# A Mamba-2 scan taken two chunks at a time, with sigmoids from the hyperbolic tangent and one logarithm per group norm

## The chip, the core and the metric

One core of a Trainium2 chip runs the whole kernel in one launch. The metric is device time in microseconds (us) of that core. "Before" is the kernel as it stood, "after" the changed one. Lines L... are lines of the kernel's file; those of before and after differ by up to some twenty.

## What is computed

A step of a two-layer network on 1024 prompt tokens and 32 new ones (together 1056; the kernel lays them out as 1060 columns, with a gap of four). Layer 0 has a Mamba-2 mixer, layer 1 latent attention; after each comes an embedding with a sigmoid gate. The mixer, which is the part that most of the change touches:

```python
def ssd_mixer(hn, conv_prev, h0, chunk, in_w, conv_w, conv_b, dt_bias, A_log, Dp, norm_w, out_w):
    proj = hn @ in_w
    z, xbc, dt = jnp.split(proj, [SSD_D_INNER, SSD_D_INNER + SSD_CONV_DIM], axis=-1)
    xbc, conv_new = causal_conv(xbc, conv_prev, conv_w, conv_b)
    xbc = jax.nn.silu(xbc)
    ...
    dt = jax.nn.softplus((dt + dt_bias).astype(F32)).reshape(b, T, SSD_GROUPS, SSD_HPG)
    A = -jnp.exp(A_log.astype(F32)).reshape(SSD_GROUPS, SSD_HPG)
    ...
    y, hT = ssd_scan(xs, dt, A, Bm, Cm, h0, chunk)
    y = y + Dp.reshape(SSD_GROUPS, SSD_HPG)[..., None] * xs
    y = y.reshape(b, T, SSD_D_INNER) * jax.nn.silu(z)
    y = rmsnorm(y.reshape(b, T, SSD_GROUPS, SSD_D_INNER // SSD_GROUPS), ...)
    out = (y @ out_w).astype(hn.dtype)
...
def ple(h, p, up_w, norm_w, gate_w):
    g = jax.nn.sigmoid((rmsnorm(h, norm_w) @ gate_w).astype(F32)).astype(h.dtype)
    return (p @ up_w).astype(h.dtype) * g
```

In the scan, with the running sums Acs of dt * A in a chunk, a chunk's own part is y_diag = (C B^T * exp(Acs_l - Acs_s) * dt, lower triangle) x, and the part from before is y_off = C h * exp(Acs); the state goes on as h * exp(Acs_last) + B^T (decay * dt * x). The kernel's chunks are of 128 tokens (eight, and the 32 new tokens as a ninth).

## The kernel before, in words

Tokens lie along the free axis, features on the partitions. float32 products are made in three parts: an operand is split into a high and a low half (h, l; wh, wl), and hh*wh, hl*wh, hh*wl are added up (`gemm`, L211 to L217). Weights come by DMA as wraw; ScalarE rounds them to wh (L206), GpSimd subtracts to wl (L207).

`phase_ssd` takes 8 groups of 4 heads. A group has six weight blocks of 128 columns: B, C, two x blocks, and two z blocks. `mblock` multiplies one block by the normalised input in three column tiles (384, 384, 292), 24 products each, so 72 products a block; ScalarE copies each tile from PSUM into a buffer raw (L335). `conv_block` makes the convolution of width 4 and SiLU from raw (ScalarE L415, VectorE three times L417, `sigmoid` L188 to L191, multiply L420). `gate` does the same for z and multiplies y by it on GpSimd (L427, L430). `scan_group` goes over the nine chunks: three transposes and C B^T into tile tr (L454 to L457), xd and xe (L464, L465), bt (L466), cbm (L467), four subtractions dm (L470), an exponential (L472), a multiply (L473), the products y_off and y_diag into yp (L477, L480), the new state st (L482), and the sums (L485 to L497). `finish` makes a group's norm, column tile by column tile: Square (L510), an add on GpSimd (L512), a split into ysh and ysl (L222, L223), two products with ones into psy (L261, L262), Ln and Exp (L182, L183), and the weighted multiply (L521).

The program's order is: blocks of group 0 and the first scan; then per group g the scan of g, the blocks B and C of g+1, the gates of g-1, x block 0 of g+1, the norm of g-1 (`finish`), x block 1 of g+1. In place of the blocks of a ninth group the last group has its gates and `up_product` for the embedding (144 products).

Ahead of it all stands the time-step chain (L358 to L404): softplus by a series on VectorE, the running sum, and nine transposes of the 96-row tile stk (pstk, L403), whose copies tokT (L404) hold dt, Acs and decay by token; every scan needs them.

The framework orders each engine's instructions once, when the kernel is built, and every engine then runs its own list in order. PSUM buffers are handed out by tag, in the order of the program: the next tile of a tag waits until the one that had its buffer has been read. Before, products (tag mm) have three banks, tr two, yp, st and "n" (the norms' sums, pstk, psy) one each.

Of the kernel before, what the change touches and what calls it, by code (L numbers as in the profile page):

```python
# [17 lines left out]
P = 128  # L18

T1 = 1060  # L20
RAWB = 7
# [133 lines left out]
class Pools:  # L155
    """tile pools by tag"""
# [29 lines left out]
def sigmoid(nc, out, x):  # L186
    """1 / (1 + exp(-x)); the cap on exp(-x) only keeps it finite"""
    nc.scalar.activation(out, x, AF.Exp, scale=-1.0)  # L188
    nc.vector.tensor_scalar(out, out, 1e30, None, op0=ALU.min)  # L189
    nc.scalar.activation(out, out, AF.Ln, bias=1.0)  # L190
    nc.scalar.activation(out, out, AF.Exp, scale=-1.0)  # L191
# [39 lines left out]
def up_product(c, i, piece, raw, tiles, ps_tile, evac, nb=1):  # L231
    """p @ W_up of layer i for one piece of the tokens, to DRAM"""
# [26 lines left out]
def ones_sum(c, ps, h, l):  # L259
    """column sums of h + l, to all rows"""  # L260
    c.nc.tensor.matmul(ps, c.ones_r, h, start=True, stop=False)  # L261
    c.nc.tensor.matmul(ps, c.ones_r, l, start=False, stop=True)  # L262


def phase_ssd(c, ctx):
# [17 lines left out]
    with tc.tile_pool(name="xin", bufs=2, side="right") as xp:  # L283
        def busy(x, k):
            """keeps the tensor engine's clock up while it waits for data; the products are not used"""
            ps = pt.tile([P, 512], F32, tag="tr", name="busy")
            for _ in range(k):
                nc.tensor.matmul(ps[:, : x.shape[-1]], c.ones, x, start=True, stop=True)

        busy(c.ones, 10)  # L290
        for j, (o, n) in enumerate(TILES1):
# [6 lines left out]
            ps = pn.tile([P, 512], F32, tag="n", name=f"psn{j}")  # L298
# [22 lines left out]
    def mblock(*blocks, ws=None):  # L321
        """products of weight blocks (source, columns, evacuation) with all tiles of hn, tile by tile"""
# [26 lines left out]
    # time steps  # L349
    with tc.tile_pool(name="dt", bufs=1) as dp:  # L350
# [57 lines left out]
    def conv_block(wsrc, b, raw=None):  # L408
# [9 lines left out]
        th = raw[:, 0:T1]  # L418
        sigmoid(nc, th, xh)
        nc.vector.tensor_tensor(xh, th, xh, op=ALU.mult)  # L420
        return xh

    def gate(g, b, S):
        z = raw_block(I["inW"][6 * g + 4 + b])[:, 3:]
        th = kp.tile([P, 3 + T1], F32, tag="raw", name="zs", bufs=RAWB)[:, 3:]
        sigmoid(nc, th, z)
        nc.gpsimd.tensor_tensor(z, th, z, op=ALU.mult)  # L427
        for j, (o, n) in enumerate(TILES1):
            yb = S["y"][j][:, b, :n]
            nc.gpsimd.tensor_tensor(yb, yb, z[:, o : o + n], op=ALU.mult)  # L430

    def scan_group(g, S):
        hT = None
        ys = S["y"] = []
        for j in range(3):
            y = wk.tile([P, 2, 384], F32, tag="y", name=f"y{j}", bufs=6)
            ys.append(y)
        nc.gpsimd.memset(ys[2][:, :, 256:260], 0.0)
        for ch in range(9):
            o, L = (ch * 128, 128) if ch < 8 else (SMP1, 32)  # L440
            j = min(ch // 3, 2)
            oy = o - TILES1[j][0]
            cs = slice(o, o + L)
            if ch == 8:
# [3 lines left out]
            ab = wk.tile([P, 4, 128], F32, tag="ab", name="ab", bufs=2)  # L448
            nc.sync.dma_start(ab[:L, :, :L], acs_d[4 * g : 4 * g + 4, cs].partition_broadcast(L))
            eb = wk.tile([P, 2, 128], F32, tag="eb", name="eb", bufs=2)  # L450
            for hf in range(2):
                nc.sync.dma_start(eb[64 * hf : 64 * hf + 64, :, :L], ea_d[4 * g + hf : 4 * g + 4 : 2, cs].partition_broadcast(64))
            tr = pt.tile([P, 512], F32, tag="tr", name="tr")
            nc.tensor.transpose(tr[:L, 0:128], S["x"][0][:, cs], c.ident)  # L454
            nc.tensor.transpose(tr[:L, 128:256], S["x"][1][:, cs], c.ident)
            nc.tensor.transpose(tr[:L, 256:384], S["B"][:, cs], c.ident)
            nc.tensor.matmul(tr[:L, 384 : 384 + L], S["B"][:, cs], S["C"][:, cs], start=True, stop=True)  # L457
            xv = tr[:L, 0:256].rearrange("p (h q) -> p h q", q=64)
            xd = wk.tile([P, 256], F32, tag="xd", name="xd", bufs=2)
            xe = wk.tile([P, 256], F32, tag="xe", name="xe", bufs=2)  # L460
            bt = wk.tile([P, 128], F32, tag="bt", name="bt", bufs=2)
            cbm = wk.tile([P, 128], F32, tag="cbm", name="cbm", bufs=2)
            hs = slice(4 * g, 4 * g + 4)
            nc.vector.tensor_tensor(xd[:L].rearrange("p (h q) -> p h q", q=64), xv, bc_last(tokT[:L, ch, 4 * g : 4 * g + 4], 64), op=ALU.mult)  # L464
# [1000 lines left out]
```

## Time and profile before

| | us |
|---|---|
| median of 3 runs | 2060.45 |
| lowest and highest run | 2057.85, 2061.4 |
| span of the profiled execution | 2062.5 |

The profiled execution has no time apart from its span. A row of a group reads: line, engine, operation, written tile <- read tiles, size, count, then busy us and mean ns of one, then idle time of the engine ahead of it and what ended most of it. A row of a timeline starts with start and length in us. "A <- B: us, n, longest" in the waits is the time that A waited for B.

### The profile page before, as it was taken

Reading aid. Unit: us, or ns where it says so; the run is one execution under the profiler, and the core shown is the slowest. Engines: PE = TensorE matmul, PEld = TensorE weight load, DVE = VectorE, ACT = ScalarE, POOL = GpSimd, SP = SyncE. Lnnn points to the kernel's source line nnn. Section 1 sums busy time; section 2 is a strip of 40 time slices with the busy share of each in tenths; the row PEclk is TensorE's granted clock in tenths of the full one; section 3 lists DMA queues with packets and bytes.
Section 4 is the critical chain, followed back from the end, with each engine's and each line's share of the span. In section 5 each row is a group of like instructions: output and inputs, shape, how many; then the busy total and the mean of one; then the engine's idle time right before and its main releaser. Section 6 shows DMA issues by size and latency. Waiting matters only on the chain. (4 is left out here: it accounts for less than half of the span.)

```text
span 2062.5 us, 33817 instructions
## 1 busy us (share of the span) xinstructions
PE 1961.9 (95%) x12871; PEld 1788.2 (87%) x12871; DVE 1426.8 (69%) x2158; ACT 1114.9 (54%) x1954; POOL 1022.9 (50%) x861
## 2 busy tenths in 40 slices
PE   7999998999999998999999899999899999989998
PEld 5988898999989997999999899877777777779998
DVE  7867888887988988435257645364679787886555
ACT  4443645456454555534244535487587767754343
POOL 5432636454563546554577544122446353655772
PEclk8999999999999999999999999999999999999999
DMA  3115253443425354735333222432612221325432
GB/s 126 52 49 109 70 107 68 93 86 78 106 61 109 64 126 126 244 118 184 102 99 120 84 70 91 144 107 84 141 29 73 60 75 32 105 64 180 132 115 79
DMA packets 141457, 204.33 MB, mean 99 GB/s; under 512 B 20272, under 2 KB 93488, under 8 KB 141168
## 3 DMA queue, kind: packets, MB, share of 16 engines
q1 hardware_dynamic: 136192, 193.18, 34.7%
q0 software_dynamic: 2800, 6.91, 1.8%
q8 instruction: 101, 1.65, 0.3%
q10 hardware_dynamic: 2304, 2.10, 0.3%
q14 instruction: 60, 0.49, 0.1%
HBM read 156.81 MB, written 38.83 MB: 95 GB/s over the span
## 5 line engine op out<-in xcount | busy, mean ns | idle before, releaser
L207 POOL TENSOR_TENSOR wl<-wraw,wh 128x1024 fp32r<-128x1024 f32 (+2 forms) x185 | 389.9, 2109 | 491.1 <-ACT wh L206 456.7
L217 PE MATMUL mm<-hh,wh 128*128 128x384 f32 (+3 forms) x1176 | 385.3, 328 | 5.4 <-ACT raw L335 5.2
L217 PE MATMUL mm<-hl,wh 128*128 128x384 f32 (+3 forms) x1176 | 388.4, 331 | 0.0
L217 PE MATMUL mm<-hh,wl 128*128 128x384 f32 (+3 forms) x1176 | 386.4, 329 | 0.0
L206 ACT ACTIVATE wh<-wraw 128x1024 fp32r<-128x1024 f32 (+3 forms) x183 | 158.7, 868 | 248.8 <-PE pso L217 124.1
L217 PE MATMUL pso<-yhl,wh 128*128 128x264 f32 x1536 | 285.0, 286 | 3.7 <-DVE yhl L223 2.0
L217 PEld LDWEIGHTS pso<-yhl,wh 128*128 128x128 f32 x1536 | 240.6, 190 | 5.0 <-DVE yhl L223 2.7
L217 PEld LDWEIGHTS mm<-hh,wh 128*128 128x128 f32 (+1 forms) x1176 | 220.9, 188 | 10.9 <-ACT raw L335 5.8
L217 PEld LDWEIGHTS mm<-hl,wh 128*128 128x128 f32 (+1 forms) x1176 | 221.2, 188 | 5.2 <-issue 2.5
L217 PEld LDWEIGHTS mm<-hh,wl 128*128 128x128 f32 (+1 forms) x1176 | 220.9, 188 | 4.7 <-issue 2.1
L217 PE MATMUL pso<-yhl,wl 128*128 128x264 f32 x768 | 219.8, 286 | 4.0 <-POOL wl L207 4.0
L217 PE MATMUL psi<-yhl,wh 128*128 128x264 f32 (+1 forms) x896 | 168.7, 289 | 4.2 <-DVE t L692 3.2
L217 PEld LDWEIGHTS pso<-yhl,wl 128*128 128x128 f32 x768 | 145.8, 190 | 4.5 <-POOL wl L207 4.5
L417 DVE SCALAR_TENSOR_TENSOR cx<-raw,pv,cx 128x1060 f32<-128x1060 f32 x96 | 141.4, 1498 | 11.6 <-ACT cx L415 11.5
L217 PE MATMUL pg<-hH,wl 128*128 128x264 f32 x512 | 146.0, 285 | 3.3 <-POOL wl L207 3.3
L217 PE MATMUL pg<-hH,wh 128*128 128x264 f32 x512 | 145.9, 285 | 0.0
L217 PE MATMUL pg<-hL,wh 128*128 128x264 f32 x512 | 145.6, 285 | 0.0
L217 PEld LDWEIGHTS psi<-yhl,wh 128*128 128x128 f32 (+1 forms) x896 | 139.3, 187 | 6.3 <-ACT lsH L222 3.2
L1228 PE MATMUL st<-qk 128*128 128x512 f32 (+2 forms) x576 | 139.6, 358 | 1.3 <-DMA qk<-mr 0.6
L217 PE MATMUL psi<-yhl,wl 128*128 128x264 f32 (+1 forms) x448 | 130.7, 292 | 2.8 <-POOL wl L207 2.8
L1249 POOL TENSOR_TENSOR pl<-pf,ph 128x512 fp32r<-128x512 f32 x64 | 81.0, 1266 | 104.0 <-DVE ph L1248 97.5
L470 DVE TENSOR_SCALAR dm<-ab,tokT 128x128 f32<-128x128 f32 (+1 forms) x288 | 120.8, 476 | 11.3 <-DMA ab<-acs_d 8.2
(522 smaller groups left out, 4866.4 us busy)
## 6 DMA issues: line engine op xcount, KB each, us to landing
wraw<-in_inW SPq DMA_DIRECT2D x48, 512.0 KB, 4.1
ab<-acs_d SPq DMA_DIRECT2D x64, 256.0 KB, 5.0
wraw<-in_outW SPq DMA_DIRECT2D x32, 512.0 KB, 3.8
yraw<-y_d SPq DMA_DIRECT2D x32, 264.0 KB, 4.6
u<-u_d SPq DMA_DIRECT2D x32, 264.0 KB, 2.7
eb<-ea_d SPq DMA_DIRECT2D x128, 64.0 KB, 3.4
wraw<-in_gateW SPq DMA_DIRECT2D x16, 512.0 KB, 3.5
wraw<-in_oW SPq DMA_DIRECT2D x16, 512.0 KB, 3.6
```

The source lines that it names most:

```text
L206: nc.scalar.activation(wh, raw, AF.Copy)
L207: nc.gpsimd.tensor_tensor(wl, raw, wh.bitcast(F32), op=ALU.subtract)
L217: c.nc.tensor.matmul(ps, ww[:, k, :m], aa, start=first and k == 0 and i == 0, stop=last and k == n - 1 and i == 2)
L417: nc.vector.scalar_tensor_tensor(xh, raw[:, k : k + T1], pvc(c, "cw", 4 * b + k), xh, op0=ALU.mult, op1=ALU.add)
L470: nc.vector.tensor_scalar(dm[:L, h, :L], ab[:L, h, :L], tokT[:L, ch, 32 + 4 * g + h : 33 + 4 * g + h], 0.0, op0=ALU.subtract, op1=ALU.min)
L1228: nc.tensor.matmul(ps[:, :n], a_[:, ks], b_[:, q], start=t == 0, stop=t == 2)
L1249: (nc.gpsimd if idx in L_POOL else nc.vector).tensor_tensor(pl[:, :n], pf[:, :n], ph[:, :n].bitcast(F32), op=ALU.subtract)
```

## The change

Four things are done:

- The scan takes chunks in pairs (`for q in range(5)`, the ninth alone). The four subtractions and the exponential of a chunk become one subtraction over 128x1024 with operands spread by broadcast, a Relu and an Exp; xd, xe, bt, cbm, the sums and the loads are made for two chunks at once. PSUM has three mm banks as before, and one bank each for trx, trb, yd, yf and st. pstk and psy, which had the bank "n", are now tiles of tag mm.
- Sigmoid and SiLU come from the hyperbolic tangent: sigmoid(x) = (1 + tanh(x/2))/2, one ScalarE pass and one VectorE operation. The halves are folded into the convolution's weights (cw, cb), the norm's weights (snw; the norm's scale becomes 1/1024) and the embedding's last operation.
- The z multiply moves from GpSimd to VectorE, and the multiply of y by z is one operation per block.
- `finish` copies the three sums into one tile r of 1060 columns and takes one Ln and one Exp over it. The tables of ScalarE's functions are loaded by ACT_TABLE_LOAD: 1 before, 30 after.

The core of the diff (the added lines of the scan without those that they replace):

```diff
-RAWB = 7
+RAWB = 6
...
-def sigmoid(nc, out, x):
-    """1 / (1 + exp(-x)); the cap on exp(-x) only keeps it finite"""
-    nc.scalar.activation(out, x, AF.Exp, scale=-1.0)
-    nc.vector.tensor_scalar(out, out, 1e30, None, op0=ALU.min)
-    nc.scalar.activation(out, out, AF.Ln, bias=1.0)
-    nc.scalar.activation(out, out, AF.Exp, scale=-1.0)
+def sigmoid2(nc, out, th, x, scale=0.5):
+    nc.scalar.activation(th, x, AF.Tanh, scale=scale)
+    nc.vector.scalar_tensor_tensor(out, th, 1.0, out, op0=ALU.add, op1=ALU.mult)
...
-    pt = es.enter_context(tc.tile_pool(name="ps_tr", bufs=2, space=bass.MemoryType.PSUM))
-    py = es.enter_context(tc.tile_pool(name="ps_y", bufs=1, space=bass.MemoryType.PSUM))
-    pst = es.enter_context(tc.tile_pool(name="ps_st", bufs=1, space=bass.MemoryType.PSUM))
-    pn = es.enter_context(tc.tile_pool(name="ps_n", bufs=1, space=bass.MemoryType.PSUM))
+    pc = es.enter_context(tc.tile_pool(name="ps_c", bufs=1, space=bass.MemoryType.PSUM))
...
-            ps = pn.tile([P, 512], F32, tag="n", name="pstk")
+            ps = mm.tile([P, 512], F32, tag="mm", name="pstk")
...
-        th = raw[:, 0:T1]
-        sigmoid(nc, th, xh)
-        nc.vector.tensor_tensor(xh, th, xh, op=ALU.mult)
+        sigmoid2(nc, xh, raw[:, 0:T1], xh, 1.0)
         return xh
     def gate(g, b, S):
         z = raw_block(I["inW"][6 * g + 4 + b])[:, 3:]
         th = kp.tile([P, 3 + T1], F32, tag="raw", name="zs", bufs=RAWB)[:, 3:]
-        sigmoid(nc, th, z)
-        nc.gpsimd.tensor_tensor(z, th, z, op=ALU.mult)
-        for j, (o, n) in enumerate(TILES1):
-            yb = S["y"][j][:, b, :n]
-            nc.gpsimd.tensor_tensor(yb, yb, z[:, o : o + n], op=ALU.mult)
+        sigmoid2(nc, z, th, z)
+        yb = S["y"][:, b]
+        nc.gpsimd.tensor_tensor(yb, yb, z, op=ALU.mult)
...
+        y = S["y"] = wk.tile([P, 2, T1], F32, tag="y", name="y", bufs=2)
...
+        for q in range(5):
+            chs = (2 * q, 2 * q + 1) if q < 4 else (8,)
+            nc_, L = (2, 128) if q < 4 else (1, 32)
+            W = nc_ * L
+            o = 256 * q if q < 4 else SMP1
+            cs = slice(o, o + W)
...
+            ex = wk.tile([P, 4, 256], F32, tag="ex", name="ex", bufs=2)[:L, :, :W]
+            nc.sync.dma_start(ex, acs_d[hs, cs].partition_broadcast(L))
+            eb = wk.tile([P, 2, 256], F32, tag="eb", name="eb", bufs=2)[:, :, :W]
             for hf in range(2):
+                nc.sync.dma_start(eb[64 * hf : 64 * hf + 64], ea_d[4 * g + hf : 4 * g + 4 : 2, cs].partition_broadcast(64))
+            trx = pc.tile([P, 2, 256], F32, tag="trx", name="trx")
+            trb = pc.tile([P, 2, 256], F32, tag="trb", name="trb")
+            for i in range(nc_):
+                cc = slice(o + L * i, o + L * i + L)
+                nc.tensor.transpose(trx[:L, i, 0:128], S["x"][0][:, cc], c.ident)
+                nc.tensor.transpose(trx[:L, i, 128:256], S["x"][1][:, cc], c.ident)
+                nc.tensor.transpose(trb[:L, i, 0:128], S["B"][:, cc], c.ident)
+            for i in range(nc_):
+                cc = slice(o + L * i, o + L * i + L)
+                nc.tensor.matmul(trb[:L, i, 128 : 128 + L], S["B"][:, cc], S["C"][:, cc], start=True, stop=True)
+            def tok(a):
+                return tokT[:L, chs[0] : chs[0] + nc_, a + 4 * g : a + 4 * g + 4]
+            xv = trx[:L, :nc_].rearrange("p c (h q) -> p c h q", q=64)
+            xd, xe = (wk.tile([P, 2, 256], F32, tag=t, name=t, bufs=2)[:L, :nc_] for t in ("xd", "xe"))
+            nc.vector.tensor_tensor(xe.rearrange("p c (h q) -> p c h q", q=64), xv, bc_last(tok(64), 64), op=ALU.mult)
+            bt = wk.tile([P, 2, 128], F32, tag="bt", name="bt", bufs=2)[:L, :nc_]
+            nc.scalar.activation(bt, trb[:L, :nc_, 0:128], AF.Copy)
+            st = pc.tile([P, 2, 256], F32, tag="st", name="st")
+            for i in range(nc_):
+                nc.tensor.matmul(st[:, i], bt[:, i], xe[:, i], start=True, stop=True)
+            nc.vector.tensor_tensor(xd.rearrange("p c (h q) -> p c h q", q=64), xv, bc_last(tok(0), 64), op=ALU.mult)
+            cbm = wk.tile([P, 256], F32, tag="cbm", name="cbm", bufs=2)[:L, :W]
+            nc.vector.tensor_tensor(cbm.rearrange("p (c l) -> p c l", c=nc_), trb[:L, :nc_, 128 : 128 + L],
+                                    bc_mid(c.tri[:L, :L], nc_), op=ALU.mult)
+            dv = ex.rearrange("p h (c l) -> p h c l", c=nc_)
+            nc.vector.tensor_tensor(dv, dv, bc_last(tok(32).rearrange("p c h -> p h c"), L), op=ALU.subtract)
+            nc.scalar.activation(ex, ex, AF.Relu, scale=-1.0)
+            nc.scalar.activation(ex, ex, AF.Exp, scale=-1.0)
+            nc.vector.tensor_tensor(ex, ex, bc_mid(cbm, 4), op=ALU.mult)
+            yd = pc.tile([P, 2, 256], F32, tag="yd", name="yd")
+            yf = pc.tile([P, 2, 256], F32, tag="yf", name="yf")
...
+            off(0)
+            for i in range(nc_):
+                for h in range(4):
+                    b, hf = h // 2, h % 2
+                    nc.tensor.matmul(yd[64 * hf : 64 * hf + 64, b, L * i : L * i + L], xd[:, i, 64 * h : 64 * h + 64],
+                                     ex[:, h, L * i : L * i + L], start=True, stop=True)
+            if nc_ == 2:
+                off(1)
...
+            t1 = wk.tile([P, 2, 256], F32, tag="t1", name="t1")
+            nc.vector.tensor_tensor(t1[:, :, f:W], yf[:, :, f:W], eb[:, :, f:W], op=ALU.mult)
+            if f:
+                nc.vector.tensor_copy(y[:, :, o : o + f], yd[:, :, :f])
+            nc.vector.tensor_tensor(y[:, :, o + f : o + W], yd[:, :, f:W], t1[:, :, f:W], op=ALU.add)
...
+    def finish(g, S):
+        y = S["y"]
+        r = wk.tile([P, T1], F32, tag="yr", name="yr")
+        for o, n in TILES1:
+            yj = y[:, :, o : o + n]
+            sq = wk.tile([P, 2, 384], F32, tag="sq", name="ysq")
+            nc.scalar.activation(sq[:, :, :n], yj, AF.Square)
+            ss = sq[:, 0, :n]
+            nc.gpsimd.tensor_tensor(ss, ss, sq[:, 1, :n], op=ALU.add)
+            sh, sl = (wk.tile([P, 384], F32R, tag=f"ys{x}", name=f"ys{x}")[:, :n] for x in "hl")
+            split(c, sh, sl, ss, eng_l=nc.gpsimd)
+            ps = mm.tile([P, 512], F32, tag="mm", name="psy")
+            ones_sum(c, ps[:, :n], sh, sl)
+            nc.scalar.activation(r[:, o : o + n], ps[:, :n], AF.Copy)
+        rsqrt(nc, c, r, r, 1.0 / 1024, c.eps)
         for b in range(2):
+            yb = y[:, b]
+            nc.vector.scalar_tensor_tensor(yb, yb, pvc(c, "snw", 2 * g + b), r, op0=ALU.mult, op1=ALU.mult)
+            c.store(c.y_d[2 * g + b][:, :1024], yb[:, :1024])
+            c.store(c.y_d[2 * g + b][:, 1024:], yb[:, SMP1:])
...
-                sigmoid(nc, tv, tv)
-                nc.vector.tensor_tensor(uv, tv, uv, op=ALU.mult)
-                nc.vector.tensor_tensor(uv, uv, hr[:, cols], op=ALU.add)
+                sigmoid2(nc, uv, tv, tv)
+                nc.vector.scalar_tensor_tensor(uv, uv, 0.5, hr[:, cols], op0=ALU.mult, op1=ALU.add)
...
+            o, n = PV["cw"]
+            nc.vector.tensor_scalar(c.pv[:, o : o + n + 32], c.pv[:, o : o + n + 32], 0.5, None, op0=ALU.mult)
+            o, n = PV["snw"]
+            nc.vector.tensor_scalar(c.pv[:, o : o + n], c.pv[:, o : o + n], 0.5, None, op0=ALU.mult)
...
+        def ln_exp():
+            tc.keep_in_program_order(nc.scalar.preload_act_table_set("natural_log_exp_and_others"))
+        ln_exp()
...
+        ln_exp()
         phase_mla_in(c, h1s, r1, tmp, yt, mt, st, latents_done)
+        ln_exp()
```

What TensorE has behind the first block's products, before (mm are products, the name behind <- the operands):

```order
L217 MATMUL mm<-hh_7_187,wh 128x292
L217 MATMUL mm<-hl_7_188,wh 128x292
L217 MATMUL mm<-hh_7_187,wl 128x292
L217 MATMUL mm<-hh_0_141,wh 128x384
L217 MATMUL mm<-hl_0_142,wh 128x384
```

And after:

```order
L215 MATMUL mm<-hh_7_178,wh 128x292
L215 MATMUL mm<-hl_7_179,wh 128x292
L215 MATMUL mm<-hh_7_178,wl 128x292
L451 MATMUL trb<-cst,cx 128x128 x2
L398 MATMUL pstk<-cst,stk 128x96 x8
L398 MATMUL pstk<-cst,stk 32x96
L215 MATMUL mm<-hh_0_132,wh 128x384
L215 MATMUL mm<-hl_0_133,wh 128x384
```

Two transposes of B and the nine of stk have moved ahead of block C of group 0. Before, the first pstk stands in the last column tile of a later block, and the nine are spread over some 200 products:

```order
L217 MATMUL mm<-hl_0_174,wh 128x292
L217 MATMUL mm<-hh_0_173,wl 128x292
L403 MATMUL pstk<-cst,stk 128x96
L217 MATMUL mm<-hh_1_175,wh 128x292
L217 MATMUL mm<-hl_1_176,wh 128x292
```

VectorE's list from the division to the end of the time-step chain, after (L412 and L189 are the convolution and SiLU of block B, the rest is the chain):

```order
L356 RECIPROCAL w<-w 32x1060
L412 SCALAR_TENSOR_TENSOR cx<-raw,pv,cx 128x1060
L357 TENSOR_TENSOR w<-w,e 32x1060
L412 SCALAR_TENSOR_TENSOR cx<-raw,pv,cx 128x1060
L358 TENSOR_TENSOR w_582<-w 32x1060
L412 SCALAR_TENSOR_TENSOR cx<-raw,pv,cx 128x1060
L359 TENSOR_SCALAR pp<-w_582 32x1060
L361 SCALAR_TENSOR_TENSOR pp<-pp,w_582 32x1060
L189 SCALAR_TENSOR_TENSOR cx<-raw,cx 128x1060
L361 SCALAR_TENSOR_TENSOR pp<-pp,w_582 32x1060 x6
L362 SCALAR_TENSOR_TENSOR pp<-pp,w 32x1060
L392 MEMSET w_582 32x4
```

Before, the part behind the fourth of these rows read so:

```order
L363 TENSOR_TENSOR w_589<-w 32x1060
L417 SCALAR_TENSOR_TENSOR cx<-raw,pv,cx 128x1060
L364 TENSOR_SCALAR pp<-w_589 32x1060
L366 SCALAR_TENSOR_TENSOR pp<-pp,w_589 32x1060
L417 SCALAR_TENSOR_TENSOR cx<-raw,pv,cx 128x1060
L366 SCALAR_TENSOR_TENSOR pp<-pp,w_589 32x1060
L189 TENSOR_SCALAR raw<-raw 128x1060
L417 SCALAR_TENSOR_TENSOR cx<-raw,pv,cx 128x1060
L366 SCALAR_TENSOR_TENSOR pp<-pp,w_589 32x1060
L417 SCALAR_TENSOR_TENSOR cx<-raw,pv,cx 128x1060
L420 TENSOR_TENSOR cx<-raw,cx 128x1060
L366 SCALAR_TENSOR_TENSOR pp<-pp,w_589 32x1060
```

There the convolutions of two more blocks stood between the steps; now the chain has the engine nearly to itself.

The norm at a group's end on TensorE, after (a steady group; trb belongs to the next group's scan, the last rows to x block 1):

```order
L215 MATMUL mm<-hh_7_178,wl 128x292
L451 MATMUL trb<-cst,cx 128x128 x2
L454 MATMUL trb<-cx 128x128
L259 MATMUL psy<-ysh,ones_r 128x384
L454 MATMUL trb<-cx 128x128
L260 MATMUL psy<-ysl,ones_r 128x384
L451 MATMUL trb<-cst,cx 128x128 x2
L454 MATMUL trb<-cx 128x128 x2
L259 MATMUL psy<-ysh,ones_r 128x384
L451 MATMUL trb<-cst,cx 128x128 x2
L454 MATMUL trb<-cx 128x128 x2
L260 MATMUL psy<-ysl,ones_r 128x384
```

It goes on with

```order
L259 MATMUL psy<-ysh,ones_r 128x292
L215 MATMUL mm<-hh_0_132,wh 128x384
L215 MATMUL mm<-hl_0_133,wh 128x384
L215 MATMUL mm<-hh_0_132,wl 128x384
L215 MATMUL mm<-hh_1_134,wh 128x384
```

Before, at the same place:

```order
L482 MATMUL st<-xe,bt 128x256
L261 MATMUL psy<-ysh,ones_r 128x384
L217 MATMUL mm<-hh_7_171,wl 128x384
L217 MATMUL mm<-hh_0_173,wh 128x292
L217 MATMUL mm<-hl_0_174,wh 128x292
L262 MATMUL psy<-ysl,ones_r 128x384
L217 MATMUL mm<-hh_0_173,wl 128x292
L217 MATMUL mm<-hh_1_175,wh 128x292
L217 MATMUL mm<-hl_1_176,wh 128x292
```

The three psy, each in two halves, stood among products and the next scan's work; now all but the last half stand ahead of x block 1, with nothing but transposes between.

GpSimd's list at a group's end, after, with the weight split wl and the convolution's small copies between the norm's steps:

```order
L528 TENSOR_TENSOR ysq<-ysq 128x384
L221 TENSOR_TENSOR ysl<-ysq,ysh 128x384
L528 TENSOR_TENSOR ysq<-ysq 128x384
L205 TENSOR_TENSOR wl<-wraw,wh 128x1024
L406 COPY raw<-pv 128x3
L407 COPY conv_c<-raw 128x3
L408 COPY conv_c<-raw 128x3
L221 TENSOR_TENSOR ysl<-ysq,ysh 128x384
L528 TENSOR_TENSOR ysq<-ysq 128x292
L221 TENSOR_TENSOR ysl<-ysq,ysh 128x292
```

Before it was:

```order
L512 TENSOR_TENSOR ysq<-ysq 128x384
L223 TENSOR_TENSOR ysl<-ysq,ysh 128x384
L488 TENSOR_TENSOR hm<-hT,cd_all 128x256
L512 TENSOR_TENSOR ysq<-ysq 128x384
L223 TENSOR_TENSOR ysl<-ysq,ysh 128x384
L488 TENSOR_TENSOR hm<-hT,cd_all 128x256
L512 TENSOR_TENSOR ysq<-ysq 128x292
L223 TENSOR_TENSOR ysl<-ysq,ysh 128x292
```

The state's multiply hm, which stood between the steps, has moved behind them, and a weight split stands there instead.

More of the change, by code (lines that the diff above doesn't have):

```diff
@@ L284, in busy @@
         def busy(x, k):
-            ps = pt.tile([P, 512], F32, tag="tr", name="busy")
+            ps = pc.tile([P, 512], F32, tag="trx", name="busy")
             for _ in range(k):
@@ L465, in scan_group @@
-            nc.vector.tensor_tensor(xe[:L].rearrange("p (h q) -> p h q", q=64), xv, bc_last(tokT[:L, ch, 64 + 4 * g : 64 + 4 * g + 4], 64), op=ALU.mult)
-            nc.scalar.activation(bt[:L], tr[:L, 256:384], AF.Copy)
-            nc.vector.tensor_tensor(cbm[:L, :L], tr[:L, 384 : 384 + L], c.tri[:L, :L], op=ALU.mult)
-            dm = wk.tile([P, 4, 128], F32, tag="dm", name="dm", bufs=2)
-            for h in range(4):
-                nc.vector.tensor_scalar(dm[:L, h, :L], ab[:L, h, :L], tokT[:L, ch, 32 + 4 * g + h : 33 + 4 * g + h], 0.0, op0=ALU.subtract, op1=ALU.min)
@@ new lines, in off @@
+            def off(i):
+                if hts[i] is not None:
+                    for b in range(2):
+                        nc.tensor.matmul(yf[:, b, L * i : L * i + L], hts[i][:, 128 * b : 128 * b + 128],
+                                         S["C"][:, o + L * i : o + L * i + L], start=True, stop=True)
+            off(0)
[4 more added lines that the diff above has]
+                                     ex[:, h, L * i : L * i + L], start=True, stop=True)
@@ L551, in phase_ssd @@
         if g:
-            for j in range(3):
-                finish(g - 1, Ss[g - 1], j)
+            finish(g - 1, Ss[g - 1])
         if g + 1 < G:
@@ L562, in phase_ssd @@
             gate(g, 1, Ss[g])
-            for j in range(3):
-                finish(g, Ss[g], j)
+            finish(g, Ss[g])
     run(up)
```

107 lines of the change are left out of this document (23 added, 84 removed).

## The prediction, made before the changed kernel ran

> **What bounds the kernel now.** I read the page first, then the busy time by stretch, then the TensorE waits of the scan. The page:
>
> ```profile
> span 2062.5 us, 33817 instructions
> ...
> PE 1961.9 (95%) x12871; PEld 1788.2 (87%) x12871; DVE 1426.8 (69%) x2158; ACT 1114.9 (54%) x1954; POOL 1022.9 (50%) x861
> ```
>
> TensorE is busy for 95% of the span. An edit on another engine is worth only what it takes from TensorE's gaps, or puts into them. The stretches (busy us of an engine, count in brackets):
>
> ```profile
> core 0: us, PE busy (x) PEld busy (x) DVE busy (x) ACT busy (x) POOL busy (x), PEclk, DMA share, GB/s
> 56.50:98.30 41.80, 41.80 (x258) 41.65 (x257) 36.60 (x26) 18.14 (x24) 19.72 (x17) 1.00 0.15 51
> 100.00:843.00 743.00, 707.05 (x4660) 664.22 (x4660) 613.43 (x1072) 397.50 (x621) 364.35 (x348) 0.99 0.44 96
> ...
> 1110.00:1156.00 46.00, 35.70 (x258) 33.88 (x256) 36.45 (x34) 22.42 (x37) 33.44 (x19) 0.92 0.32 104
> ```
>
> From 100 to 843 us (the eight groups) TensorE lacks 743.0 - 707.1 = 36 us. VectorE is busy 83% there, TensorE 95%. In the stretch where the first embedding gate hands over to attention (1110 to 1156) it lacks 10.3. What it waits for in the scan, in total, times, longest:
>
> ```profile
> PE tr L454 <- DVE cbm L467: 9.2, 8, 2.7
> PE tr L455 <- DVE cx L420: 7.5, 4, 3.3
> PE mm L217 <- ACT raw L335: 4.2, 2, 3.2
> ```
>
> Small waits on VectorE, up to some 3 us each. Removing all of them is worth 36 us; that caps the gain of everything that makes the scan's element work cheaper.
>
> **The start.** What stands on TensorE behind the first block now starts with the nine transposes of stk. They have taken tag mm's slots ahead of block C of group 0, whose products now wait for the whole time-step chain. Before, 257 products ran there without a gap (56.5 to 98.3 above: 41.80 of 41.80 busy):
>
> ```profile
> 56.39 0.30 PE L217 MATMUL mm<-hh,wl 128*128 128x292 f32 x1
> 56.52 0.34 PE L217 MATMUL mm<-hh,wh 128*128 128x384 f32 x1
> ```
>
> The chain's prices (mean ns of one) and the start of its long division:
>
> ```profile
> 58.11 6.77 DVE L361 RECIPROCAL w<-w 32x1060 f32<-32x1060 f32 x1
> ```
>
> ```profile
> L417 DVE SCALAR_TENSOR_TENSOR cx<-raw,pv,cx 128x1060 f32<-128x1060 f32 x13 | 19.0, 1465 | 5.2 <-ACT cx L415 5.1
> L366 DVE SCALAR_TENSOR_TENSOR pp<-pp,w 32x1060 f32<-32x1060 f32 x7 | 10.8, 1543 | 0.0
> ...
> L420 DVE TENSOR_TENSOR cx<-raw,cx 128x1060 f32<-128x1060 f32 x3 | 3.7, 1238 | 0.0
> ...
> L390 DVE COPY stk<-acs 32x1060 f32<-32x1060 f32 x1 | 2.8, 2782 | 0.0
> L381 DVE TENSOR_TENSOR_SCAN acs<-msk,w 32x1060 f32<-32x1060 f32 x1 | 2.3, 2347 | 0.0
> ...
> L367 DVE SCALAR_TENSOR_TENSOR pp<-pp,w 32x1060 f32<-32x1060 f32 x1 | 1.2, 1244 | 0.0
> ...
> L375 DVE TENSOR_SCALAR w<-stk,aneg 32x1060 f32<-32x1060 f32 x1 | 0.8, 754 | 0.0
> ```
>
> ```profile
> L398 ACT ACTIVATE w<-w 32x1060 f32<-32x1060 f32 x1 | 1.1, 1092 | 3.0 <-DVE w L396 3.0
> ```
>
> ```profile
> L404 DVE COPY tokT<-pstk 128x96 f32<-128x96 f32 x8 | 2.0, 252 | 3.6 <-PE pstk L403 3.6
> ```
>
> From 58.11: the division 6.77; thirteen operations of about line 367's kind (lines 362, 363, seven of 366, 367, 371, 392, 399) at 1.24, 16.1; line 364, priced as 375, and 375 1.5; scan 2.35; copy 2.78; line 398 1.09: 30.6. Between them VectorE's new order has only four convolution operations of block B: three at 1.47 and the new SiLU multiply, priced as line 420, 1.24: 5.6. So stk stands at 58.1 + 36.2 = 94.3. Seven of the nine copies come before the slot that block C needs: 7 x 0.25 = 1.8. Products restart at 96.1 instead of 56.5: **39.5 us**, bounds 37 (adjacent operations overlap a little) and 42 (line 366 at its mean of 1.54). Nothing covers this: TensorE's queue is in order, and behind the waiting transposes stand the 216 products of blocks C, x0 and x1; for these wait the evictions on ScalarE, the convolutions on VectorE and with them the first group's scan, so the whole program moves back. Behind such a wait the clock is granted by half:
>
> ```profile
> 46.40:53.30 6.90, 5.80 (x24) 0.51 0.00 1
> ```
>
> Here 6.9 us at 0.51 lost 3.4 (us, busy, granted clock). I add 3, bounds 0 and 5. The Trainium skill, "TensorE: Matmul & The Clock Gate", Part 1, gives the warm-up as one window of about 3.4 us; that would cost 1.7 here, and this row shows twice the window, so the row decides.
>
> **The end of a group.** psy has lost its bank and shares tag mm. It comes in the middle of x block b=1's turn, so this block stands behind psy 0 to 2, and the next group's trb work is interleaved. Before, products were spread between them. The steps of a psy are serial, as sq, ysh and ysl have one buffer each:
>
> ```profile
> L207 POOL TENSOR_TENSOR wl<-wraw,wh 128x1024 fp32r<-128x1024 f32 x44 | 124.6, 2832 | 144.8 <-ACT wh L206 143.3 <-ACT ex L472 1.5
> ...
> L512 POOL TENSOR_TENSOR ysq<-ysq 128x384 f32<-128x384 f32 x15 | 16.5, 1100 | 3.6 <-ACT ysq L510 3.6
> L223 POOL TENSOR_TENSOR ysl<-ysq,ysh 128x384 fp32r<-128x384 f32 x15 | 16.0, 1065 | 4.5 <-ACT ysh L222 3.8 <-PE mm L217 0.7
> ```
>
> ```profile
> L510 ACT ACTIVATE ysq<-y 128x768 f32<-128x768 f32 x15 | 12.7, 844 | 15.3 <-POOL y L430 9.9 <-POOL ysl L223 5.4
> ...
> L222 ACT ACTIVATE ysh<-ysq 128x384 fp32r<-128x384 f32 x15 | 7.9, 524 | 16.5 <-POOL ysq L512 14.4 <-POOL raw L410 2.1
> ```
>
> One step is ysl 1.07, square 0.84, add 1.10, ysh 0.52: 3.5 us; two steps stand between psy 0 and psy 2, 7.1. GpSimd's order puts one wl (2.83) between the second add and the second ysl, the ScalarE order a 1060-wide convolution start ahead of the third square. That makes some 10 us. TensorE has about 2.5 us of transposes and psy there, and the other products that could fill it stand behind. From 2 (the POOL chain started well before TensorE arrived) to 9 per group; I take **6, six times: 36**. The wide Ln and Exp with their table loads stand behind on ScalarE beside x block b=1: nothing, while this block's products last.
>
> **The pairs.** VectorE's work falls: per group 32 of the first row go for four of double the second:
>
> ```profile
> L470 DVE TENSOR_SCALAR dm<-ab,tokT 128x128 f32<-128x128 f32 x256 | 108.5, 480 | 11.3 <-DMA ab<-acs_d 8.2 <-ACT ex L472 2.9 <-ACT raw L335 0.2
> L473 DVE TENSOR_TENSOR ex<-ex,cbm 128x512 f32<-128x512 f32 x64 | 68.9, 1081 | 1.6 <-ACT ex L472 0.5
> ```
>
> 15.4 against 4 x 2.16 = 8.6, with the sigmoid's cap some 9 us a group. But it frees VectorE under TensorE's cover; TensorE gains only from shorter waits. Against that, trx, trb, yd, yf and st have one bank each: the next pair's transposes wait for all readers of this pair's, and the readers are twice as long (a multiply of 2.16 holds up yd). I count 0 to 4 us a group and take **2, eight times: 16**.
>
> **The tail of the scan.** The last up-products (144) stand behind psy of group 7, and that behind the last gate. Before they covered it. Beside the rows above:
>
> ```profile
> L427 POOL TENSOR_TENSOR raw<-zs,raw 128x1060 f32<-128x1060 f32 x16 | 41.1, 2572 | 54.7 <-ACT zs L191 54.7
> ```
>
> ```profile
> L188 ACT ACTIVATE zs<-raw 128x1060 f32<-128x1060 f32 x16 | 17.4, 1088 | 0.9 <-DVE hT L490 0.7
> ```
>
> From the last gate product: tanh 1.1, multiply 1.2, the wide gate product (as 427) 2.6, square 0.8, add 1.1, ysh 0.5, two steps 7.1: 14.4, with hand-overs and eviction 17; group 6's finish 5: **22**, bounds 10 and 30.
>
> **Edits at nothing.** Each convolution block loses two ScalarE passes of 1.09 and trades VectorE's cap and multiply for one operation; the z product goes from GpSimd (2.57) to VectorE; the y product becomes one of the same length in all; six Ln and Exp of a group become three copies, one Ln and one Exp. All of it lies under TensorE's products in the stretch 100 to 843, where ScalarE is at 53% and GpSimd at 49%; if that cover were gone, it would show as shorter waits, and these are taken off in full below. The two operations that halve constants come in the first microseconds, beside loads. One raw buffer less can hold back an eviction, and with it an mm slot: the row of mm behind raw above is the nearest, 4.2 us in all; I leave it inside the pairs' bound. The merged broadcast loads (72 to 40 and 144 to 80 issues) keep their bytes and pass fewer times through SP's queue; the one wait on them (8.2 us in line 470's row) is VectorE's, under cover.
>
> **Gains.** The 36 us of old waits are replaced by the terms above, so all are taken off. At 1110 to 1156 the sigmoid loses two of four steps, and these were the largest wait there:
>
> ```profile
> ACT t L190 <- DVE t L189: 14.4, 6, 2.8
> ```
>
> I take 6 of the 10.3 (bounds 2 and 10.3). The chain of waits at the end has seven operations behind the last product, and will have four:
>
> ```profile
> 2057.70 0.31 DVE t L189
> 2058.01 0.02 issue
> 2058.03 0.43 ACT t L190
> ```
>
> Three at 0.3 to 0.45: 1.3.
>
> **Sum** on the profiled execution: 39.5 + 3 + 36 + 16 + 22 = 116.5 added, 36 + 6 + 1.3 = 43.3 taken: +73. Its span of 2062.5 lies 2 above the median of the runs (2060.45). 2060.5 + 73 = 2133.5, rounded **2133 us**.
>
> **Rivals.** (a) *Only the start costs.* VectorE's relief shortens the chains at the groups' ends and in the pairs so far that the scan waits as much as before, 36 us, and no more: 42.5 - 7.3 = +35, 2096. For it: with 8 x 9 us less, VectorE's 83% become 73%. Against: the psy steps are on GpSimd and ScalarE. (b) *Faster: the relief takes every wait of the scan.* Start 37 without a clock loss, the 36 and 10.3 + 1.3 gone: -11, 2050. It decides where all new waits at groups' ends, pairs and tail together stay below 7 us, against 74 in my sum. (c) *ScalarE is put on the path* by the added loads of activation tables, two per group's end. The trace has one load:
>
> ```profile
> L1333 ACT ACT_TABLE_LOAD x1 | 1.3, 1283 | 0.7 <-PEq L1447 0.7
> ```
>
> Two of 1.28 and a wide Ln and Exp at 1.09 each are 4.7; if x block b=1's evictions wait for them in full, 8 x 4.7 = 38 more: 2171. The Trainium skill, "ScalarE: Activation LUTs", "What ACT_TABLE_LOAD costs", gives 2.66 us with the drain, by which it would be 8 x 7.5 = 60: 2193; the row agrees on the 1283 ns, and no run here shows the drain. (d) *The start's wait isn't there*, since something else fills TensorE: +33, 2094; the order speaks against it.
>
> **How the numbers follow.** Forecast 0.77, (a) 0.10, (b) 0.06, (c) 0.05, (d) 0.02. The forecast's own bounds, taken as independent (start 5, groups' ends 24, pairs 16, tail 12), are about +-31: 2102 to 2164. To hold 8 in 10 with (a) the range is **2080 to 2168**. A measurement here tells 0.2% (4 us) from no change. Faster 0.06, same 0.03, slower 0.91.
>
> **What would show it.** A TensorE gap from 56 to 96 us that ends with a copy of pstk (line 399 after); gaps at 2 to 9 us in front of psy, six times, with ysh or ysl as releaser; waits of trx and trb on VectorE; 15 to 20 us before the last up-products. If TensorE's busy time between the first group and 900 us is over 97%, the terms for groups' ends and pairs were wrong. If ScalarE's table loads end waits of mm products, it is (c).

## The result, and the profile after

| | us |
|---|---|
| before, median of 4 runs | 2060.9 (2057.85 to 2069.6) |
| after, median of 4 runs | 2129.5 (2126.1 to 2129.7) |
| after / before | 1.0327, 95% interval 1.0299 to 1.0355 |
| span of the profiled execution after | 2124.3 |

The change makes the kernel 3.3% slower. The three runs of before in the first table are among these four. All times of runs are device times; readings inside a run are from its one profiled execution. The page of after, with busy time and share of each engine:

```profile
span 2124.3 us, 32594 instructions
...
PE 1965.5 (93%) x12871; PEld 1801.1 (85%) x12871; DVE 1273.0 (60%) x1607; ACT 1032.3 (49%) x1757; POOL 938.3 (44%) x813
```

VectorE, ScalarE and GpSimd each have less to do (154, 83 and 85 us less), TensorE has the same matmuls, and its gaps are wider. The stretches of after (busy us of TensorE, count, granted clock):

```profile
56.40:94.50 38.10, 2.93 (x12) 0.54 0.14 38
94.50:98.50 4.00, 4.00 (x16) 0.68 0.69 111
135.00:262.00 127.00, 126.74 (x893) 1.00 0.39 91
262.00:274.00 12.00, 10.70 (x70) 1.00 0.14 45
274.00:278.00 4.00, 1.49 (x11) 0.99 0.14 27
278.00:282.00 4.00, 2.47 (x10) 0.50 0.26 104
282.00:286.00 4.00, 4.00 (x17) 0.65 0.00 0
286.00:290.00 4.00, 4.00 (x25) 1.00 0.00 0
800.00:912.00 112.00, 81.36 (x506) 0.86 0.46 144
```

Three things are to be seen: an empty stretch at the start, a dense one while the first pairs run, and at a group's end (262 to 290) 5.4 us of waiting with the clock at half behind it. The start in TensorE's timeline:

```profile
92.18 2.27 PE L398 MATMUL pstk<-cst,stk 96*128 96x96 f32 x9 [17.16 <-DVE stk L394]
94.47 0.69 PE L215 MATMUL mm<-hh,wh 128*128 128x384 f32 x1
```

Products begin again at 94.5, when stk (VectorE L394) is through. The waits of TensorE from 262 to 800 us, which hold six groups' ends:

```profile
PE trb L451 <- DVE cbm L469: 23.6, 12, 2.4
PE psy L259 <- ACT ysh L220: 7.9, 6, 1.5
PE psy L260 <- POOL ysl L221: 1.2, 3, 0.4
```

These are 33 us, 5.4 at each group's end, and they are all the waits there; away from the ends, TensorE waits for nothing in the pairs. The waits at one of these ends, the products of x block 1 behind them (first, and where they get shorter), and the operations on VectorE and ScalarE that the first wait goes back to:

```profile
274.75 0.44 PE L451 MATMUL trb<-cst,cx 128*128 128x128 f32 x2 [2.06 <-DVE cbm L469]
277.58 0.44 PE L451 MATMUL trb<-cst,cx 128*128 128x128 f32 x2 [1.76 <-DVE cbm L469]
278.50 0.69 PE L260 MATMUL psy<-ysl,ones_r 128*128 128x384 f32 x1
280.71 0.61 PE L259 MATMUL psy<-ysh,ones_r 128*128 128x292 f32 x1 [1.53 <-ACT ysh L220]
281.12 0.53 PE L215 MATMUL mm<-hh,wh 128*128 128x384 f32 x1
284.64 0.40 PE L215 MATMUL mm<-hh,wl 128*128 128x384 f32 x1
284.88 0.34 PE L215 MATMUL mm<-hh,wh 128*128 128x384 f32 x1
```

```profile
274.27 0.42 DVE L469 TENSOR_TENSOR cbm<-trb,cst 128x256 f32<-128x256 f32 x1 [8.60 <-ACT bt L463]
```

```profile
273.87 0.37 ACT L463 ACTIVATE bt<-trb 128x256 f32<-128x256 f32 x1
```

Two of the three waits stand ahead of the next pair's trb: its one bank is free only when cbm has read it, and cbm came behind bt. GpSimd at the same end, with what it waits for:

```profile
272.80 0.99 POOL L528 TENSOR_TENSOR ysq<-ysq 128x384 f32<-128x384 f32 x1 [0.95 <-ACT ysq L526]
273.75 2.35 POOL L205 TENSOR_TENSOR wl<-wraw,wh 128x1024 fp32r<-128x1024 f32 x1
276.05 1.18 POOL L406 COPY raw<-pv 128x3 f32<-128x3 f32 x1
277.18 0.18 POOL L407 COPY conv_c<-raw 128x3 f32<-128x3 f32 x1
277.30 0.18 POOL L408 COPY conv_c<-raw 128x3 f32<-128x3 f32 x1
277.44 1.00 POOL L221 TENSOR_TENSOR ysl<-ysq,ysh 128x384 fp32r<-128x384 f32 x1
```

The second split ysl waits 3.7 us behind the weight split and the small copies, and the third psy, with all of x block 1 behind it, waits for what follows. ysl is done at 278.44 and its psy starts at 278.50, so without the waits for trb TensorE would have had to wait for ysl instead; this is read from the rows and was not tried by itself. The tail, on TensorE:

```profile
873.12 0.69 PE L259 MATMUL psy<-ysh,ones_r 128*128 128x384 f32 x1 [11.50 <-ACT ysh L220]
874.20 0.69 PE L260 MATMUL psy<-ysl,ones_r 128*128 128x384 f32 x1 [0.39 <-POOL ysl L221]
877.06 0.69 PE L259 MATMUL psy<-ysh,ones_r 128*128 128x384 f32 x1 [2.17 <-ACT ysh L220]
878.13 0.69 PE L260 MATMUL psy<-ysl,ones_r 128*128 128x384 f32 x1 [0.39 <-POOL ysl L221]
880.21 0.61 PE L259 MATMUL psy<-ysh,ones_r 128*128 128x292 f32 x1 [1.39 <-ACT ysh L220]
```

15.8 us of waiting ahead of the last up-products. The first output product (pso) starts at 911.7, before at 842.4: the scan is 69.3 us longer. What follows takes 2124.3 - 911.7 = 1212.6, before 2062.5 - 842.4 = 1220.1: 7.5 shorter.

### The profile page after: what moved, and what is told of

It is laid out like the page before. It is cut to its first block, busy times and chain, and to the rows that moved or that the text cites. A ratio compares the mean times of both kernels' runs of the same rounds, so it can differ in the third digit from the quotient of the medians.

```text
span 2124.3 us, 32594 instructions
## 1 busy us (share of the span) xinstructions
PE 1965.5 (93%) x12871; PEld 1801.1 (85%) x12871; DVE 1273.0 (60%) x1607; ACT 1032.3 (49%) x1757; POOL 938.3 (44%) x813
## 5 line engine op out<-in xcount | busy, mean ns | idle before, releaser
L205 POOL TENSOR_TENSOR wl<-wraw,wh 128x1024 fp32r<-128x1024 f32 (+2 forms) x185 | 364.1, 1969 | 592.7 <-ACT wh L204 528.2
L412 DVE SCALAR_TENSOR_TENSOR cx<-raw,pv,cx 128x1060 f32<-128x1060 f32 x96 | 132.5, 1380 | 45.5 <-ACT cx L410 44.0
L487 POOL TENSOR_TENSOR hm<-hT,cd_all 128x256 f32<-128x256 f32 x64 | 63.0, 985 | 170.8 <-DVE hT L489 125.1
```

The source lines that it names most:

```text
L205: nc.gpsimd.tensor_tensor(wl, raw, wh.bitcast(F32), op=ALU.subtract)
L412: nc.vector.scalar_tensor_tensor(xh, raw[:, k : k + T1], pvc(c, "cw", 4 * b + k), xh, op0=ALU.mult, op1=ALU.add)
L487: nc.gpsimd.tensor_tensor(hm.rearrange("p (h q) -> p h q", q=64), hT.rearrange("p (h q) -> p h q", q=64), bc_last(cd_all[:, hs, ch], 64), ...
```

## The experiments

Theory: the places of pstk and psy in tag mm, whose slots go in program order, hold up products that have nothing to do with them; the new element operations cost nothing. Rivals: the waits only move (1), the norm's chain is late wherever psy stands (2), pairs or table loads cost time themselves (3). All twelve runs, below after itself; each ratio is to the kernel before as timed beside that run:

| kernel | median us | after / before it, 95% |
|---|---|---|
| after | 2129.5 | 1.030 to 1.036 |
| after, pstk off mm | 2104.7 | 1.020 to 1.023 |
| after, psy off mm | 2044.9 | 0.991 to 0.994 |
| after, both off mm | 2024.4 | 0.980 to 0.984 |
| before, pstk in mm | 2060.8 | 0.9995 to 1.002 |
| before, psy in mm | 2121.2 | 1.028 to 1.032 |
| both off mm, three logarithms | 2050.5 | 0.994 to 0.997 |
| both off mm, old sigmoid | 2027.6 | 0.983 to 0.987 |
| both off mm, tanh only behind the scan | 2017.8 | 0.979 to 0.982 |
| that, with three logarithms | 2018.8 | 0.978 to 0.982 |
| before, short wait | 2046.8 | 0.991 to 0.996 |
| both off mm, short wait | 2026.8 | 0.982 to 0.987 |
| before, another order | 2045.4 | 0.992 to 0.995 |

**pstk off mm.**

```diff
-            ps = mm.tile([P, 512], F32, tag="mm", name="pstk")
+            ps = pc.tile([P, 512], F32, tag="st", name="pstk")
```

> After, with the nine transposes of stk in tag st's bank in place of tag mm; nothing else. Theory (the slots' order makes block C wait for the time-step chain): TensorE's gap of 38 us between 56 and 94.5 us goes, and the time falls by 36 to 40, to 2090 to 2094. Rival 1 (the wait only moves: the first scan needs tokT in any case): the gap turns up in front of the first scan, and the time stays above 2115.

The gap is gone, but the time fell by 25, not 38, and lies between the two expectations. TensorE's busy time from 100 to 300 us went from 194.4 (after) to

```profile
100.00:300.00 200.00, 180.64 (x1218) 0.97 0.34 84
```

so 13.8 us of waiting came up in the first two groups, most of it on VectorE. Rival 1 has a third of the wait, the theory two thirds. The first scan (its first xe on VectorE) starts at 141.7 us, at 147.8 in after: 6 us earlier, although the products are 38 us ahead.

**psy off mm.**

```diff
-            ps = mm.tile([P, 512], F32, tag="mm", name="psy")
+            ps = pc.tile([P, 512], F32, tag="st", name="psy")
```

> After, with psy in tag st's bank in place of tag mm; pstk stays in mm. Theory: the waits ahead of psy and of trb at six groups' ends (33 us) and most of those ahead of psy in the tail (25 us) go: 45 to 58 less, 2072 to 2085, with the gap from 56 to 94 us unchanged. Rival 2 (the chain of square, add and split is late itself, and products run out for its sake): under 15 less, above 2114.

It fell by 85, more than expected, and rival 2 is out. From the restart to the end of the scan, TensorE in after and then in this version:

```profile
94.50:911.70 817.20, 753.47 (x4910) 0.95 0.34 90
```

```profile
94.50:835.00 740.50, 728.73 (x4917) 1.00 0.37 96
```

Idle time falls from 63.7 to 11.8, by 52, which is the expected term. The other 24.7 are busy time: the same products took longer under the half clock that follows each wait. In the rows of 278 to 286 above that is 2.47 x 0.50 + 4.00 x 0.35 = 2.6 us of busy time at one group's end, 16 at six; the other 9 fit the tail, where TensorE was busy for 81.4 us at a granted 0.86.

**Both off mm** (both edits).

> After, with pstk and psy in tag st's bank. Theory: the two terms add up, 83 to 98 less: 2032 to 2047, faster than before by 0.7 to 1.4%, since all that the change was to relieve then shows. Rival 3 (the pairs or ScalarE's 30 table loads cost something of their own that the two waits cover): 2060 or more.

2024.4: 105 less than after, the sum of 25 and 85 but for some 4, and 1.8% faster than before. Rival 3 is out for this version. From the first block's end to the first output product, TensorE before and in this version:

```profile
56.50:842.40 785.90, 749.99 (x4923) 0.99 0.42 93
```

```profile
56.50:813.00 756.50, 730.25 (x4922) 1.00 0.36 96
```

Its idle time falls from 35.9 us to 26.3 only; two thirds of the 29.4 us gained here are shorter busy time for the same products (those of the state st alone 38.6 us in place of 49.8, and a granted clock of 1.00 in place of 0.99). The prediction's cap on the gain, 36 us of waits, left out that the products' own time changes.

**The two places put into the kernel before.** pstk first, psy second:

```diff
-            ps = pn.tile([P, 512], F32, tag="n", name="pstk")
+            ps = mm.tile([P, 512], F32, tag="mm", name="pstk")
```

> Before, with the nine transposes of stk in tag mm and nothing else. Theory: the start's wait by itself, 36 to 42 us more than before, less up to 8 for the waits of before around 104 to 165 us, which the early tokT takes away: 2089 to 2103. Rival 1: within 10 us of before, 2061 to 2071.

```diff
-        ps = pn.tile([P, 512], F32, tag="n", name="psy")
+        ps = mm.tile([P, 512], F32, tag="mm", name="psy")
```

> Before, with the norms' sums psy in tag mm and nothing else. Theory (the slots' order puts x block 1 behind the serial steps of a norm): idle TensorE and half clock of some 8 us at six groups' ends and some 25 in the tail, less the old waits that fall into them: 30 to 70 more, 2090 to 2130. Rival 2: under 15 more, below 2075.

psy in mm costs 60, as expected, on a scan of single chunks with the old sigmoid: the place does it, whatever the element operations are. pstk in mm costs nothing measurable, as rival 1 had it and against the theory, although its gap is there:

```profile
92.36 2.27 PE L403 MATMUL pstk<-cst,stk 96*128 96x96 f32 x9 [35.64 <-issue]
```

All of it is paid back. Up to the first output product (841.7 us, before 842.4) TensorE's other waits come to 9.7 us, before to 35.9, and its busy time to 739.9, before 750.0. From 300 to 800 us it is busy 495.9 of 500 us in this version,

```profile
300.00:800.00 500.00, 495.90 (x3331) 1.00 0.43 88
```

and in the kernel before only

```profile
300.00:800.00 500.00, 481.56 (x3218) 1.00 0.43 87
```

The first scan hardly moves: before, its first operation on VectorE (xd) starts at 149.9 us, behind the last of the nine copies tokT at 149.7; here the last copy starts at 94.7 and xd at 152.5. The products come 36 us later, the scan 2.6.

**Why is it paid back?** Two runs ask it of the kernel before: a shorter pause, and new lists without a pause.

```diff
         nc.vector.tensor_tensor(w2, w, w, op=ALU.mult)
+        gap = mm.tile([P, 512], F32, tag="mm", name="gap")
+        nc.tensor.transpose(gap[:, :32], w2[:, 0:128], c.ident[:32, :32])
```

> Before, with one unused transpose of the time-step chain's square (line 363) in a tile of tag mm behind block 0: a wait of TensorE of about 12 us near 57 us, and nothing else. It asks why the 36 us of pstk in mm cost the kernel before nothing. Head start (VectorE's backlog at the start feeds the later waits, so that a pause of TensorE is paid back): 2054 to 2064, with a gap of 10 to 14 us near 57 and less waiting from 100 us on. No head start (the longer wait only happened to come with a better order): 2068 to 2075.

```diff
-            nc.vector.scalar_tensor_tensor(xh, raw[:, k : k + T1], pvc(c, "cw", 4 * b + k), xh, op0=ALU.mult, op1=ALU.add)
+            i = nc.vector.scalar_tensor_tensor(xh, raw[:, k : k + T1], pvc(c, "cw", 4 * b + k), xh, op0=ALU.mult, op1=ALU.add)
+            if k == 1 and raw is first:
+                tc.keep_in_program_order(i)
```

> Before, with the first convolution operation of block B pinned in VectorE's order behind what was written ahead of it, so that the time-step chain comes a little earlier; no wait of TensorE is added, and all lists are built anew. Head start (a pause of TensorE at the start is what is paid back): as before, 2055 to 2066. Order (the lists of before are merely worse than others that the same scheduling gives): 2052 or less, or above 2070.

A pause of 13.1 us made the kernel 14 us *faster*: outside both expectations. New lists without a pause also made it faster, by 12, as the order theory had it. From 300 to 800 us the short pause leaves TensorE 494.9 us busy, the new lists alone 485.3. So the two versions with a pause run dense later and the two without don't, which speaks for a head start of VectorE; but an order alone is worth 12 us too, and every edit rebuilds all lists. The start of the first scan doesn't settle it either: the short pause brings its first xd to 129.0 us, 20.9 earlier than before, and the new lists to 154.0, 4.1 later, though their time-step chain comes 15 us earlier (the copy of the running sums into stk at 95.8 against 111.2). The causes aren't separated.

The same short wait in the version with both off mm:

> The version with pstk and psy off tag mm, with the unused transpose of the time-step chain's square in tag mm behind block 0 (a wait of TensorE of 11 to 14 us near 57 us). If such a pause is paid back here too (this version waits 14 us between 100 and 300 us): 2012 to 2026. If the pairs leave VectorE nothing to catch up: 2032 to 2040.

2026.8 against 2024.4, just above the first range: paid back but for 2 (from 100 to 300 us TensorE is busy 196.9 us, without the pause 187.1), and no gain.

**What the parts of the change are worth.** On the version with both off mm, first one logarithm per column tile, then the old sigmoid everywhere:

```diff
-            nc.scalar.activation(r[:, o : o + n], ps[:, :n], AF.Copy)
-        rsqrt(nc, c, r, r, 1.0 / 1024, c.eps)
+            rsqrt(nc, c, r[:, o : o + n], ps[:, :n], 1.0 / 1024, c.eps)
```

> The version with pstk and psy off tag mm, with one Ln and one Exp for each column tile of the norm, as before (62 table loads in place of 30). Theory (ScalarE's loads lie under TensorE's products): within 6 of that version's 2024.4, so 2018 to 2031. Rival (c) of the prediction (table loads on the path): 32 more loads of 1.28 us and the smaller Ln and Exp come through, 2045 or more.

```diff
-    nc.scalar.activation(th, x, AF.Tanh, scale=scale)
-    nc.vector.scalar_tensor_tensor(out, th, 1.0, out, op0=ALU.add, op1=ALU.mult)
+    nc.scalar.activation(th, x, AF.Exp, scale=-2.0 * scale)
+    nc.vector.tensor_scalar(th, th, 1e30, None, op0=ALU.min)
+    nc.scalar.activation(th, th, AF.Ln, bias=1.0)
+    nc.scalar.activation(th, th, AF.Exp, scale=-1.0)
+    nc.vector.scalar_tensor_tensor(out, th, 2.0, out, op0=ALU.mult, op1=ALU.mult)
```

> The version with pstk and psy off tag mm, with the sigmoid of before (Exp, cap, Ln, Exp, then the multiply) in every place; 3 table loads. Theory: in the scan the extra passes lie under TensorE's products, and only the 7.5 us gained behind the scan (embeddings, latents, the end) come back: 2029 to 2040. Rival: the relief of ScalarE and VectorE is what makes the scan dense: 2050 or more.

Three logarithms cost 26: the theory missed. By the two profiles 16.8 us of it lie in the scan (first pso at 829.8, with one logarithm 813.0), where TensorE's idle time rises from 26.3 to 39.3 us; 5.2 lie behind the scan, where this edit changes nothing. The old sigmoid costs 3, just below the theory's range, and by the first pso the scan itself is shorter with it (804.8 against 813.0); what follows is longer by 6.7. So the tangent was put behind the scan alone, with the old sigmoid under another name in `conv_block` and `gate`:

```diff
-        sigmoid2(nc, xh, raw[:, 0:T1], xh, 1.0)
+        sigmoid_exp(nc, xh, raw[:, 0:T1], xh, 1.0)
...
-        sigmoid2(nc, z, th, z)
+        sigmoid_exp(nc, z, th, z)
```

> The version with pstk and psy off tag mm, with the sigmoid of before in the convolutions and gates of the scan, and the hyperbolic tangent only behind the scan (embeddings, latents' gate); 12 table loads. Theory: the scan as in the version with the old sigmoid everywhere (8 us shorter by its profile), and the 7 us behind the scan kept: 2012 to 2020, the best of all. Rival: the scans of these two differ by chance of the order only, and it lies between them, 2021 to 2029.

2017.8, within the theory's range; the scan is 6.4 us shorter by the first pso (806.6 against 813.0). But an edit without work moved before by 12 us, and the two versions' intervals in the table overlap, so that the tangent costs anything inside the scan isn't shown. And this version with three logarithms again, where no other table is needed in the scan:

> The version with pstk and psy off tag mm and the old sigmoid in the scan, with one Ln and one Exp for each column tile of the norm. Nothing in the scan needs another function table then: 12 loads, as without this edit. It asks what the 26 us were that three logarithms cost beside the hyperbolic tangent. The loads themselves: 2012 to 2024, as with one logarithm (2017.8). The more and shorter Ln and Exp, or the sums' banks held longer: 2035 or more.

2018.8: without table loads three logarithms cost nothing. So the 26 us go with the loads; their size is less sure, since rebuilt lists move the time too. ScalarE at a group's end in the version with the tangent and three logarithms:

```profile
347.27 1.28 ACT L182 ACT_TABLE_LOAD   x1
348.56 0.58 ACT L182 ACTIVATE yr<-psy,eps 128x384 f32<-128x384 f32 x1
349.16 1.28 ACT L183 ACT_TABLE_LOAD   x1
350.45 0.53 ACT L183 ACTIVATE yr<-yr 128x384 f32<-128x384 f32 x1
```

Four operations of 3.7 us stand where two of 1.1 would do, and what follows in ScalarE's list queues behind them: in the scan TensorE waits 6.3 us ahead of psy for yr, with one logarithm 0.8. One logarithm per norm is worth something only beside the tangent; with the old sigmoid the scan needs no further load.

## Why the prediction was right, point by point

It said 2133 (2080 to 2168), slower, and 2129.5 was measured. The direction and the places were right. That the sum came so near is in part luck, as two terms that it lacked went against each other. By the two profiled executions the kernel is 61.8 longer, against 73 forecast; by the medians 69; the profiled execution of after was the fastest of its four.

- **The start**, 39.5 without products: 38.1. stk was ready some 2 us earlier than worked out, because its copy, priced at 2.78, took 0.70. Half clock behind it, 3: the stretch 94.5 to 98.5 was granted 0.68, which is 1.3 over these 4 us. But the step "so the whole program moves back" was wrong in its worth: the first scan starts at 147.8 us in after and at 149.9 in before. Taking the gap away gave 25 in after, and putting it into the kernel before cost nothing, since there later waits got shorter. The prediction had no term for that; what pays the pause back stays open.
- **The groups' ends**, 6 each, 36: 5.4 each, 33. Of these, 9.1 stand ahead of psy behind ysh and ysl, as it said, and 23.6 ahead of trb behind VectorE, which it had named as a sign of the pairs; both go with psy off mm, so the place of psy brings both about. It left out the half clock behind each of these ends, some 2.6 us. It had a term for this behind the start and none elsewhere; psy off mm gave back 24.7 us of longer products, the tail's included.
- **The pairs**, 2 each, 16: nothing beside products, where one bank each for trx, trb, yd, yf and st holds nothing up: 126.7 of 127 us busy from 135 to 262. At the groups' ends, where no products stand beside it, the one bank of trb shows in the 23.6 us above.
- **The tail**, 22: the waits ahead of psy are 9.3 for group 6 (0.7, 2.4 and 6.2) and 15.8 for group 7, 25 together; the whole stretch 800 to 912 lost 30.6.
- **Gains**: 7.3 behind the scan, 7.5 measured. The 36 us of old waits were taken off in full, and after has none of them between 135 and 262. This isn't the relief alone: with both off mm, and so without the pause at the start, 26.3 us of idle time remain in the scan.
- **Sum over the scan**: +80.5 forecast, +69.3 measured: 62.9 more idle time (98.8 against 35.9 us) and 6.4 more busy time (756.4 against 750.0). The half clock that the forecast left out, 24.7, was nearly made up by the shorter busy time of the pairs, which it left out too (731.6 with psy off mm, 18.4 less than before).
- **Table loads** at nothing: they end no wait of TensorE in after between 262 and 800, but the cover is thin: twice as many, with psy and pstk off mm, cost 26 us.
- **The clock, the loads and the Trainium skill**: at the group's end above the products restart behind the last wait at 281.12 us, take 0.53 each until 284.6 and 0.34 from 284.9: 3.6 us at half clock (the psy at 278.50, ahead of that wait, was at half clock already). The Trainium skill's warm-up window of about 3.4 us ("TensorE: Matmul & The Clock Gate", Part 1) agrees with this row. It doesn't fit every wait: at the start the products are back to 0.34 us 2.7 us after they begin at 94.47, and in the row of 46.4 to 53.3 that the prediction quoted they run at half clock for 5.8 us, from 47.5. The Trainium skill's 2.66 us for a load with its drain ("ScalarE: Activation LUTs", "What ACT_TABLE_LOAD costs") doesn't agree with the rows of ScalarE: there the function starts 1.29 us after its load does, and the load 0.02 us after the function ahead of it ends.

## What to carry to other kernels

Where buffers of a tag are handed out in program order, a small tile that comes late stops every product behind it: give tiles with a late producer a bank of their own or one that only their readers share, and look at the bound engine's list for what stands behind them. A function that saves a pass but needs another table has to be counted with its loads: here 32 more of them cost 26 us, and inside the scan the tangent showed no gain (2024.4, with the old sigmoid there 2017.8). Before a few microseconds are put down to an edit, note that one which added neither work nor a wait moved this kernel by 12.

## What was not expected of the hardware

- A wait of TensorE of some 5 us costs some 2.6 more in half clock behind it, which the profile books as busy time: 24.7 us in this scan, the tail's included.
- One operation of the time-step chain, a 32x1060 copy on VectorE, took 2.78 us before and 0.70 after. Before, GpSimd's weight split (2.43 us) ran from 111.0 beside it (111.2); after, GpSimd had no operation on tiles at that time. All fourteen traces agree: 2.77 to 2.81 us in the six in which a weight split runs beside this copy, and 0.70 in the eight in which none does. It wasn't tried by itself.
